# FFN weights of a decoder block: most loaded straight into SBUF with a cast instead of being converted in DRAM first, and bias sums placed ahead of their expansion

## The chip, the cores and the metric

The kernel runs on all eight cores of one Trainium2 chip, one batch element a core. The metric is the device time of the slowest core in microseconds (us). Cores 0 to 3 are one die, cores 4 to 7 the other. The profiles name the engines PE (TensorE, the matmuls), PEld (its weight loads), DVE (VectorE), ACT (ScalarE), POOL (GpSimd) and SP (SyncE).

Some executions fall into a slower state: one die shows a lower granted TensorE clock and runs more than 1% longer than the other, or the time is more than 1.5% above the fastest of that kernel. These executions are marked slow, and only fast ones are compared here.

## The reference, cut to what matters

```python
# BATCH 8, SEQ 2048, D_MODEL 1024, D_FF 4096; all float32
h = rms_norm(x, norm_mix_pre)
u_a, v_a, q, k, v_b, g_a, g_b = split(h @ w_in)
# branch A: chunked spatial gating, 8 groups of 128 channels, chunks of 128 tokens
v   = layer_norm(gelu(v_a), ln_v_g, ln_v_b)
y_a = gelu(u_a) * (tril(w_s) @ v  per chunk and group  + b_s)
# branch B: y_b = dilated sliding-window attention (untouched by the change)
merged = sigmoid(g_a + b) * (y_a @ w_a_proj) + sigmoid(g_b + b) * (y_b @ w_b_proj)
x = x + rms_norm(merged @ w_out)                      # "output projection"
x = x + rms_norm(relu(rms_norm(x) @ w_ff1)**2 @ w_ff2)   # FFN: FF1, then FF2
```

Of the kernel before, what the change touches and what calls it, by code (L numbers as in the profile page):

```python
# [9 lines left out]
BF16 = mybir.dt.bfloat16  # L10
AF = mybir.ActivationFunctionType
ALU = mybir.AluOpType
# [346 lines left out]
def build_nc():  # L359
    nc = bass.Bass("TRN2", target_bir_lowering=False)  # L360
# [21 lines left out]
    vscr_d = nc.dram_tensor("v_scr", [4, 4, 128, 4, 384], BF16).ap()  # L382
    x1_d = nc.dram_tensor("x1_scr", [16, 128, DM], F32).ap()
    gscr_d = nc.dram_tensor("gc_scr", [16, 128, 1024], BF16).ap()
    w1s_d = nc.dram_tensor("w1_bf", [8, 128, 4096], BF16).ap()
    w2s_d = nc.dram_tensor("w2_bf", [16, 128, 2048], BF16).ap()

    es = ExitStack()
    P = Plan(nc, es)
    psall = es.enter_context(nc.psum_tensor("pst", [128, 8, 512], F32))  # L390

    def ps(b):
        return psall[:, b, :]
# [6 lines left out]
    def buf(name, off, shape, dt=BF16):  # L400
        return Buf(P, name, int(off), shape, dt)
# [101 lines left out]
    for i in range(2):  # L503
        P.dve(lambda e, i=i: e.memset(stg[i][:, :, :, 64:128], 1.0), 2048, [], [stg[i].key()], prio=-1950 + i)


    def conv_items():
        its = []
        for f in range(2, 8):
            its.append(lambda f=f: P.dma("pool", lambda e: e.dma_start(out=w1s_d[f], in_=w1_d[f]), 3e6, f"cv{f % 2}", [], [P.nkey(("w1s", f))], after=anchor[0]))  # L510
        for f in range(16):
            its.append(lambda f=f: P.dma("pool", lambda e: e.dma_start(out=w2s_d[f], in_=w2_d[f]), 1.5e6, f"cv{f % 2}", [], [P.nkey(("w2s", f))], after=anchor[0]))
        return its

# [192 lines left out]

    conv = conv_items()
    nconv = len(conv)
    proj_qk(0, lambda i, n: -1990.0 + 20 * i)  # L710
# [26 lines left out]
    wva = buf("wva", 144 * K, [8, 1024])  # L737
    wu = [buf(f"wu{i}", (128 + 2 * i) * K, [8, 128]) for i in range(8)]
    Rx = buf("Rx", 160 * K, [8, 512], F32)
# [75 lines left out]
    for hf in range(2):  # L815
        P.pe([(ps(4 + hf), onesf[:], wsTf[:, 512 * hf:512 * hf + 512], True, True, 2048, False)], [onesf.key(), wsTf.key()], [4 + hf])
        for gi in range(4):
            g = 4 * hf + gi
            o = Rx[:, g, :].rearrange("p (t b m) -> p t b m", t=16, b=4)
            P.dve(lambda e, g=g, gi=gi, hf=hf: e.scalar_tensor_tensor(  # L820
                out=BS[:, 128 * g:128 * g + 128], in0=ps(4 + hf)[:, 128 * gi:128 * gi + 128], scalar=small[:, lb_c + g:lb_c + g + 1],
                in1=BS[:, 128 * g:128 * g + 128], op0=ALU.mult, op1=ALU.add), 128, [ksm, BS.key()], [BS.key((128 * g, 128 * g + 128))], [4 + hf])
            P.dve(lambda e, g=g, o=o: e.tensor_copy(
                out=o, in_=BS[:, 128 * g:128 * g + 128].rearrange("p (t m) -> p t m", t=16).unsqueeze(2).broadcast_to([128, 16, 4, 8])), 512,
                [BS.key((128 * g, 128 * g + 128))], [Rx.key(g)])

# [6 lines left out]
    for g in range(8):  # L833
# [8 lines left out]
        anchor[0] = P.ops[-1]  # L842
        conv.pop(0)()
        for n4 in range(4):
# [24 lines left out]

    def load_w1(f, prio):  # L870
        src = w1_d if f < 2 else w1s_d
        P.dma("pool", lambda e: e.dma_start(out=w1[f][:].rearrange("p k c -> p (k c)"), in_=src[f]), 1e6 if f > 1 else 2e6, f"w1_{f}",
              [P.nkey(("w1s", f))], [w1[f].key()], prio=prio)
    for cb in range(8):
# [9 lines left out]
        for w in range(4):  # L884
# [8 lines left out]
            anchor[0] = P.ops[-1]  # L893
            if conv and cb >= 1 and it % 3:
                P.prio = G0 + 20 * cb + 5 * w + 2
                conv.pop(0)()
            P.prio = G0 + 20 * cb + 5 * w
            s_ = sg[it % 2]
# [73 lines left out]

    for f in range(2, 8):
        load_w1(f, F0 + 4 * (f - 2))
    for q in range(16):
        P.dma("pool", lambda e, q=q: e.dma_start(out=w2[:, 2 * q:2 * q + 2, :].rearrange("p f c -> p (f c)"), in_=w2s_d[q]), 0.5e6, f"w2_{q}",
              [P.nkey(("w2s", q))], [w2.key((2 * q, 2 * q + 2))], prio=F0 + 20 + q, after=fgate[q])
    assert not conv
    gfin = buf("gfin", 200 * K, [1024], F32)
# [5 lines left out]
    for w in range(4):  # L985
        for fb in range(32):
            P.prio = L0 + 100 * w + fb
            f, f4 = fb // 4, fb % 4
            bk = (6, 7)[fctr[0] % 2]
            fctr[0] += 1  # L990
            P.pe([(ps(bk), w1[f][:, kc, 128 * f4:128 * f4 + 128], h2T[:, kc, 512 * w:512 * w + 512], kc == 0, kc == 7, 512, False)
                  for kc in range(8)], [w1[f].key(), h2T.key(None, (512 * w, 512 * w + 512))], [bk], name="ff1")
            P.act(lambda e, fb=fb, bk=bk: e.activation(out=hid[:, fb, :], in_=ps(bk), func=AF.Relu), 512, [], [hid.key(fb)], [bk])  # L993
            P.dve(lambda e, fb=fb: e.tensor_tensor(out=hid[:, fb, :], in0=hid[:, fb, :], in1=hid[:, fb, :], op=ALU.mult), 512, [hid.key(fb)],  # L994
                  [hid.key(fb)], rate=2)
# [116 lines left out]
```

## The kernel before: the parts that the change and the argument touch

A small planner (`P`) records every operation with a priority, and each engine then executes its operations in a fixed order. `P.dma("pool", ...)` goes into GpSimd's queue, which carries every transfer with a cast here; `P.dma("sp", ...)` goes into SyncE's queue. `after=op` holds a transfer back until that operation is done.

The FFN weights w1 (8 chunks, each 1 MB in bf16) and w2 (16 chunks, each 0.5 MB in bf16) arrive as f32. Chunks 2 to 7 of w1 and all of w2, 22 in all, are first converted from DRAM to DRAM and later loaded as bf16:

```python
for f in range(2, 8):
    its.append(lambda f=f: P.dma("pool", lambda e: e.dma_start(out=w1s_d[f], in_=w1_d[f]), ..., after=anchor[0]))
for f in range(16):
    its.append(lambda f=f: P.dma("pool", lambda e: e.dma_start(out=w2s_d[f], in_=w2_d[f]), ..., after=anchor[0]))
```

The stage before gating computes v for 16 tiles of 128 tokens. Each LayerNorm result goes through one of three `gct` buffers into a DRAM scratch, and from there a gather turns it into `gc`, 8 partitions a tile. Both are in SyncE's queue:

```python
for n in range(16):
    ...  # v_a matmuls on PE, gelu on ACT, statistics and normalisation on DVE/POOL
    t_ = gct[n % 3]
    P.dve(... out=t_ ...)
    P.dma("sp", ... e.dma_start(out=gscr_d[n], in_=t_[:]) ...)                       # store, 256 KB
for n in range(16):
    P.dma("sp", ... e.dma_start(out=gc[8*n:8*n+8, :, :],
                                in_=gscr_d[n].rearrange("(b m) c -> m b c", m=8)) ...)   # gather, 256 KB
```

The bias sums `BS` free the PSUM banks 4 and 5, which the first u matmuls need. Each sum was followed by its expansion into `Rx`:

```python
for g in ...:
    P.dve(... scalar_tensor_tensor(out=BS[g], in0=ps(4 + hf)..., in1=BS[g]) ...)
    P.dve(... tensor_copy(out=Rx[g], in_=BS[g] broadcast) ...)
```

Then come u, gating and merge. One conversion is issued per u group, and the other 14 in the merge:

```python
for g in range(8):
    for w in range(4):
        ...                                     # u matmuls, gelu
    anchor[0] = P.ops[-1]
    conv.pop(0)()                               # one conversion
    for n4 in range(4):
        P.prio = U0 + 10 * (g + 3) + 5 + n4     # gating matmuls run about three u groups later
        P.pe(... gc x wsT ...)
for cb in range(8):                             # merge
    P.dma("pool", ... wb <- wg_d[cb], prio=G0 + 20 * cb - 30)
    if cb == 1: ...                             # four loads of w_out
    for w in range(4):
        ...                                     # 32 matmuls
        if conv and cb >= 1 and it % 3: conv.pop(0)()
```

The output projection works through 16 tiles, each with a load of x (512 KB), 16 matmuls, an RMSNorm, a store of x1 (512 KB) and a transpose for the FFN. The bf16 FFN weights are loaded meanwhile:

```python
for i in range(16):
    P.dma("sp", ... x_ <- x[i])                 # two buffers
    ...
    P.dma("sp", ... x1_d[i] <- x_)
for f in range(2, 8): load_w1(f, F0 + 4 * (f - 2))
for q in range(16):   P.dma("pool", ... w2[q] <- w2s_d[q], after=fgate[q])   # after projection tile q
```

The softmax here doesn't subtract the row's maximum and nothing guards it: scores larger than these inputs give would overflow.

## Time and profile before

| | before |
|---|---|
| time, median of 3 runs | 1314.57 us (1313.46 to 1316.37) |
| spans of the eight cores in the profiled execution | 1299.2 to 1318.6 us |
| mean granted TensorE clock of the cores | 0.963 to 0.969 |
| first v_a matmul to first gating matmul, mean of the cores | 185.8 us |
| first gating matmul to first matmul of the projection | 258.7 us |
| first matmul of the projection to first FF2 matmul | 141.4 us |
| first FF2 matmul to the end | 394.3 us |

The last four rows cut the kernel at points that every core has, taken from the trace's records of single matmuls; all cores reach the first v_a matmul at 324 to 329 us. FF1 of the first window begins before the first FF2 matmul, so the third row contains a little of the FFN.

First the table by stage, kernel before, core 3 (the slowest). Each row is a stretch of time; its columns are the length, then the busy us and the instruction count of PE, PE's weight loads, VectorE, ScalarE and GpSimd, then the granted TensorE clock, the mean busy share of the 16 DMA engines, and GB/s.

```profile
core 3: us, PE busy (x) PEld busy (x) DVE busy (x) ACT busy (x) POOL busy (x), PEclk, DMA share, GB/s
415.00:440.00 25.00, 13.42 (x55) 5.40 (x53) 5.38 (x10) 4.94 (x9) 1.96 (x5) 0.80 0.75 132
...
450.00:475.00 25.00, 20.27 (x94) 9.02 (x92) 5.53 (x10) 7.46 (x13) 5.48 (x12) 0.98 0.94 167
475.00:500.00 25.00, 0.00 (x0) 0.00 (x0) 0.00 (x0) 0.00 (x0) 0.00 (x0) 0.50 0.85 126
500.00:517.00 17.00, 0.00 (x0) 0.00 (x0) 0.00 (x0) 0.00 (x0) 0.00 (x0) 0.50 0.44 81
564.00:780.00 216.00, 216.00 (x1004) 97.92 (x1002) 70.77 (x105) 42.65 (x63) 13.38 (x26) 1.00 0.57 91
780.00:900.00 120.00, 99.72 (x524) 46.18 (x523) 75.86 (x123) 66.55 (x185) 9.66 (x18) 0.96 0.73 245
924.00:1255.00 331.00, 329.95 (x1528) 149.43 (x1528) 73.77 (x156) 78.05 (x168) 0.00 (x0) 1.00 0.11 39
```

PE is full in the merge (564 to 780) and in the FFN (924 to 1255). From 475 to 517 it does nothing at all, while the DMA engines are 85% and then 44% busy. The projection (780 to 900) leaves it idle for 20 us of 120.

The chain of work that ended last, same core, tells what the idle time waits for. Columns: start, duration, what.

```profile
414.55 23.25 DMA gc_scr<-sb_gct_127
...
438.86 9.48 DMA gc_scr<-sb_gct_127
448.88 12.46 DMA gc_scr<-sb_gct_129
461.82 39.22 DMA gc_scr<-sb_gct_128
...
501.17 0.27 SPq L808
501.52 7.13 DMA gc_scr<-sb_gct_127
508.78 8.31 DMA sb_gc<-gc_scr
...
786.00 7.54 DMA x_scr<-sb_xo_159
793.66 5.49 DMA sb_xo_159<-x
```

`gc_scr<-sb_gct` are stores of 256 KB; one of them took 39.22 us. The stretch in which PE stands still runs from this store to `sb_gc<-gc_scr`, the last gather. The three buffers explain only a part of why one store follows the other: for the last store (501.52) VectorE had its tile ready at 472.25 (timeline of core 3). The waits of PE from 385 to 565 us on core 3 (total us, times, longest) put numbers on it:

```profile
PE pst L195 <- DMA sb_gc<-gc_scr: 47.3, 1, 47.3
PE pst L195 <- ACT sb_gv_125 L787: 11.3, 2, 10.3
PE pst L195 <- DVE sb_BS L820: 9.0, 1, 9.0
```

PE waits 47.3 us for the gathers, 10.3 us at once for a gelu (held up, through the gct buffers, by a store), and 9.0 us for the bias sums. From 764 to 935 us, in the projection, its wait for a tile of x is small:

```profile
PE pst L195 <- DVE sb_xo_159 L950: 3.9, 2, 2.1
```

### The profile page before, as it was taken

The page shows a single profiled execution, that of the slowest core. Times are in us where ns is not written, and L with a number is a line of the kernel's source. Part 1 is how long each engine was busy: PE and PEld are TensorE (multiplying, and loading weights), DVE is VectorE, ACT ScalarE, POOL GpSimd, SP SyncE. Part 2 cuts the span into 40 slices and gives each one's busy share as a digit, 9 for nine tenths or more (in the row PEclk, how much of TensorE's full clock was granted, in tenths as well). Part 3 has the DMA queues.
Part 4 walks back from the last instruction along what each step waited for, and adds up shares of the span by engine and source line. Part 5 has one row for each costly group of instructions (what it writes and reads, how often), then busy time and mean ns, then how long its engine had stood idle before and what let it go on. Part 6 is the DMA issues. An engine that isn't in the chain of part 4 may idle for free.

```text
span 1318.6 us, 20421 instructions; the slowest of 8 cores (1299.2 to 1318.6 us)
## 1 busy us (share of the span) xinstructions
PE 1174.5 (89%) x7560; PEld 591.2 (45%) x7560; DVE 579.4 (44%) x997; ACT 509.6 (39%) x878; POOL 59.8 (5%) x120
## 2 busy tenths in 40 slices
PE   4799999998985722999999987899999999999997
PEld 2466666554542311544444443444444444444443
DVE  5767777877655401653223336672122113113212
ACT  5357778878643210211221134563123113212311
POOL 0000000000012100000000000010000000000000
PEclk9899999999998865999999998999999999999999
DMA  9474434344118693698645336664020020011001
GB/s 238 130 172 89 91 70 110 87 108 82 25 51 161 127 156 60 84 143 126 96 81 86 75 113 228 218 226 173 33 86 11 9 89 33 0 64 65 1 32 64
DMA packets 63555, 128.32 MB, mean 97 GB/s; under 512 B 37153, under 2 KB 37281, under 8 KB 60962
## 3 DMA queue, kind: packets, MB, share of 16 engines
q0 software_dynamic: 9440, 52.43, 22.5%
q1 hardware_dynamic: 54018, 74.58, 19.4%
q8 instruction: 62, 1.02, 0.3%
q14 instruction: 35, 0.29, 0.1%
HBM read 137.48 MB, written 41.94 MB: 136 GB/s over the span
## 4 chain that ended last, share of the span: by engine, by line
PE 75%; DMA 14%; ACT 4%; DVE 4%; issue 3%; SPq 0%; DVEq 0%; ACTq 0%
PE pst L195 75%; DMA gc_scr<-sb_gct_128 4%; DMA gc_scr<-sb_gct_127 3%; DMA sb_xo_159<-x 2%; DMA sb_xo_160<-x 1%; DMA sb_gc<-gc_scr 1%; DMA gc_scr<-sb_gct_129 1%; DMA sb_xt_87<-x 1%; DMA sb_xt_89<-x 1%; ACT sb_Et_84 L628 1%; DMA sb_wva<-w_va 1%; DMA x_scr<-sb_xo_159 1%; ACT sb_Et_83 L628 1%; ACT sb_Lr_86 L699 0%; PE pst L199 0%
## 5 line engine op out<-in xcount | busy, mean ns | idle before, releaser
L195 PE MATMUL pst<-sb_w_157,sb_hid 128*128 128x512 bf16 x1024 | 221.7, 379 | 2.7 <-DVE sb_hid L994 1.4
L195 PEld LDWEIGHTS pst<-sb_w_157,sb_hid 128*128 128x128 bf16 x1024 | 100.0, 98 | 124.0 <-issue 3.7
L993 ACT ACTIVATE sb_hid<-pst 128x512 bf16<-128x512 f32 x128 | 76.3, 596 | 127.0 <-PE pst L195 126.7
L994 DVE TENSOR_TENSOR sb_hid<-sb_hid 128x512 bf16<-128x512 bf16 x128 | 54.2, 424 | 131.3 <-ACT sb_hid L993 128.8
L1007 ACT ACTIVATE sb_junk_173<-pst 128x512 bf16<-128x512 f32 x32 | 19.1, 598 | 197.3 <-PE pst L195 197.3
L195 PE MATMUL pst<-sb_wva,sb_hT 128*128 128x512 bf16 x256 | 60.8, 391 | 14.9 <-ACT sb_gv_125 L787 11.3
L195 PE MATMUL pst<-sb_wout,sb_merged 128*128 128x512 bf16 x256 | 61.8, 398 | 7.2 <-DVE sb_xo_159 L950 3.9
L195 PE MATMUL pst<-sb_hT,sb_wqk_62 128*128 128x512 bf16 x256 | 65.3, 404 | 0.9 <-DVE sb_hT L496 0.9
L628 ACT ACTIVATE sb_Et_82<-pst 128x1024 bf16<-128x1024 f32 (+1 forms) x54 | 52.4, 970 | 26.3 <-PE pst L195 19.7
L195 PE MATMUL pst<-sb_hT,sb_wqk_63 128*128 128x512 bf16 x256 | 60.4, 380 | 0.0
L195 PE MATMUL pst<-sb_hT,sb_wg_140 128*128 128x512 bf16 x256 | 58.4, 379 | 0.0
L195 PE MATMUL pst<-sb_hT,sb_wg_141 128*128 128x512 bf16 x256 | 57.9, 379 | 0.0
L628 ACT ACTIVATE sb_Et_83<-pst 128x1024 bf16<-128x1024 f32 (+1 forms) x53 | 51.9, 980 | 8.3 <-PE pst L195 4.8
L628 ACT ACTIVATE sb_Et_84<-pst 128x1024 bf16<-128x1024 f32 (+1 forms) x53 | 51.5, 972 | 9.3 <-PE pst L195 6.1
L195 PE MATMUL pst<-sb_wsT,sb_gc 128*128 128x128 bf16 x128 | 9.9, 230 | 47.9 <-DMA sb_gc<-gc_scr 47.3
L840 ACT ACTIVATE sb_yaT<-pst 128x512 bf16<-128x512 f32 x32 | 19.1, 597 | 86.4 <-PE pst L195 86.4
L195 PEld LDWEIGHTS pst<-sb_wva,sb_hT 128*128 128x128 bf16 x256 | 24.3, 100 | 46.2 <-issue 21.0
L195 PEld LDWEIGHTS pst<-sb_wout,sb_merged 128*128 128x128 bf16 x256 | 25.4, 102 | 40.1 <-issue 14.3
L900 ACT ACTIVATE sb_sg_0_145<-pst,sb_small 128x512 f32<-128x512 f32 x16 | 11.0, 688 | 73.1 <-PE pst L195 65.8
L195 PEld LDWEIGHTS pst<-sb_hT,sb_wqk_62 128*128 128x128 bf16 x256 | 24.2, 103 | 33.0 <-issue 12.1
L852 DVE SCALAR_TENSOR_TENSOR sb_tmpm_131<-pst,sb_small,sb_Rx 128x512 bf16<-128x512 f32 x16 | 12.0, 748 | 61.2 <-PE pst L195 61.2
L195 PEld LDWEIGHTS pst<-sb_hT,sb_wg_141 128*128 128x128 bf16 x256 | 25.1, 98 | 30.2
(402 smaller groups left out, 1961.7 us busy)
## 6 DMA issues: line engine op xcount, KB each, us to landing
w_bf<-w POOLq DMA_DIRECT2D x16, 512.0 KB, 12.0
sb_w_157<-w_bf POOLq DMA_DIRECT2D x16, 512.0 KB, 6.2
w_bf<-w POOLq DMA_DIRECT2D x6, 1024.0 KB, 27.4
sb_xo_159<-x SPq DMA_DIRECT2D x8, 512.0 KB, 6.5
sb_gc<-gc_scr SPq DMA_DIRECT2D x16, 256.0 KB
sb_xo_160<-x SPq DMA_DIRECT2D x8, 512.0 KB, 6.1
sb_wg_140<-w_g POOLq DMA_DIRECT2D x4, 1024.0 KB, 12.8
sb_wg_141<-w_g POOLq DMA_DIRECT2D x4, 1024.0 KB, 10.2
```

The costliest lines, as they stand in the source:

```text
L195: e.matmul(out, lhsT=l, rhs=r, start=st, stop=sp, skip_group_check=True))
L628: P.act(lambda e: e.activation(out=et[:, :, 0:W], in_=psall[:, sb:sb + 2, 0:W], func=AF.Exp, scale=0.125), 2 * W, [], [et.key()], [sb, sb ...
L840: P.act(lambda e, bk=bk, g=g, w=w: e.activation(out=yaT[:, g, 512 * w:512 * w + 512], in_=ps(bk), func=AF.Gelu_apprx_tanh), 512, [], [yaT. ...
L852: P.dve(lambda e, bk=bk, g=g, tm=tm: e.scalar_tensor_tensor(out=tm[:], in0=ps(bk), scalar=small[:, lg_c + g:lg_c + g + 1], in1=Rx[:, g, :] ...
L900: P.act(lambda e, j=j, cb=cb, po=po, s_=s_: e.activation(out=s_[j][:], in_=ps(po + j), func=AF.Tanh, scale=0.5, bias=small[:, bg_c + 8 * j ...
L993: P.act(lambda e, fb=fb, bk=bk: e.activation(out=hid[:, fb, :], in_=ps(bk), func=AF.Relu), 512, [], [hid.key(fb)], [bk])
L994: P.dve(lambda e, fb=fb: e.tensor_tensor(out=hid[:, fb, :], in0=hid[:, fb, :], in1=hid[:, fb, :], op=ALU.mult), 512, [hid.key(fb)], [hid.k ...
L1007: P.act(lambda e, hf=hf, bb=bb, s_=s_: e.activation(out=junk4[:, 0:512], in_=ps(bb[hf]), func=AF.Square, accum_out=s_[:, 8 + hf:9 + hf]), ...
```

## The change

The intent was to take conversions out of the stage before gating, where the stores of gct seemed to suffer from them. Chunks 2, 3, 4 of w1 and 0 to 9 of w2 are loaded from f32 into SBUF with the cast, during the output projection. Only nine chunks (w1 5 to 7, w2 10 to 15) are still converted in DRAM, in the merge. The last six w2 chunks are loaded in the first FF1 pass. All BS sums come early, and the copies into Rx later; the places of the u weights in SBUF are permuted to suit.

```diff
-        conv.pop(0)()                                   # in the u/gating loop
+    conv = []
+    for f in range(3):  conv.append(... w1s_d[f] <- w1_d[5 + f] ...)
+    for q in range(6):  conv.append(... w2s_d[q] <- w2_d[10 + q] ...)
...
-            if conv and cb >= 1 and it % 3:             # merge
+            if conv and cb >= 1 and it % 2:
...
-    for f in range(2, 8):
-        load_w1(f, F0 + 4 * (f - 2))                    # bf16
-    for q in range(16):
-        P.dma("pool", ... w2[q] <- w2s_d[q], prio=F0 + 20 + q, after=fgate[q])
+    for n, f in enumerate((2, 3, 4)):
+        load_w1(f, F0 + 8 * n, fgate[n])                # f32, cast
+    for q in range(10):
+        load_w2(q, F0 + 24 + q, fgate[3 + q])           # f32, cast
+    for f in (5, 6, 7):
+        load_w1(f, F0 + 40 + f)                         # bf16
...
+            if w == 0 and fb >= 18 and fb < 24:         # first FF1 pass
+                load_w2(fb - 8, P.prio, P.ops[-1])      # bf16
...
             P.dve(... scalar_tensor_tensor(out=BS[g] ...)
-            P.dve(... tensor_copy(out=Rx[g], in_=BS[g]))
+                prio=M0 + 2)
+    for g in range(8):
+        P.dve(... tensor_copy(out=Rx[g], in_=BS[g]) ..., prio=M0 + 70 + g)
```

More of the change, by code (lines that the diff above doesn't have):

```diff
@@ L383, in build_nc @@
     x1_d = nc.dram_tensor("x1_scr", [16, 128, DM], F32).ap()
+    w1s_d = nc.dram_tensor("w1_bf", [3, 128, 4096], BF16).ap()
+    w2s_d = nc.dram_tensor("w2_bf", [6, 128, 2048], BF16).ap()
     gscr_d = nc.dram_tensor("gc_scr", [16, 128, 1024], BF16).ap()
-    w1s_d = nc.dram_tensor("w1_bf", [8, 128, 4096], BF16).ap()
-    w2s_d = nc.dram_tensor("w2_bf", [16, 128, 2048], BF16).ap()
     es = ExitStack()
@@ L504, in build_nc @@
         P.dve(lambda e, i=i: e.memset(stg[i][:, :, :, 64:128], 1.0), 2048, [], [stg[i].key()], prio=-1950 + i)
-    def conv_items():
-        its = []
-        for f in range(2, 8):
-            its.append(lambda f=f: P.dma("pool", lambda e: e.dma_start(out=w1s_d[f], in_=w1_d[f]), 3e6, f"cv{f % 2}", [], [P.nkey(("w1s", f))], after=anchor[0]))
-        for f in range(16):
-            its.append(lambda f=f: P.dma("pool", lambda e: e.dma_start(out=w2s_d[f], in_=w2_d[f]), 1.5e6, f"cv{f % 2}", [], [P.nkey(("w2s", f))], after=anchor[0]))
-        return its
     T = 100.0
@@ L706, in pv_class @@
                   [ybT.key(hp, (512 * c, 512 * c + 512), rows=(lo, lo + 64))], [bks[hh]], name="norm")
-    conv = conv_items()
-    nconv = len(conv)
     proj_qk(0, lambda i, n: -1990.0 + 20 * i)
@@ L737, in build_nc @@
     wva = buf("wva", 144 * K, [8, 1024])
-    wu = [buf(f"wu{i}", (128 + 2 * i) * K, [8, 128]) for i in range(8)]
+    wu = [buf(f"wu{i}", o * K, [8, 128]) for i, o in enumerate((132, 134, 140, 142, 128, 130, 136, 138))]
     Rx = buf("Rx", 160 * K, [8, 512], F32)
@@ L818, in build_nc @@
             g = 4 * hf + gi
-            o = Rx[:, g, :].rearrange("p (t b m) -> p t b m", t=16, b=4)
             P.dve(lambda e, g=g, gi=gi, hf=hf: e.scalar_tensor_tensor(
                 out=BS[:, 128 * g:128 * g + 128], in0=ps(4 + hf)[:, 128 * gi:128 * gi + 128], scalar=small[:, lb_c + g:lb_c + g + 1],
-                in1=BS[:, 128 * g:128 * g + 128], op0=ALU.mult, op1=ALU.add), 128, [ksm, BS.key()], [BS.key((128 * g, 128 * g + 128))], [4 + hf])
-            P.dve(lambda e, g=g, o=o: e.tensor_copy(
-                out=o, in_=BS[:, 128 * g:128 * g + 128].rearrange("p (t m) -> p t m", t=16).unsqueeze(2).broadcast_to([128, 16, 4, 8])), 512,
-                [BS.key((128 * g, 128 * g + 128))], [Rx.key(g)])
+                in1=BS[:, 128 * g:128 * g + 128], op0=ALU.mult, op1=ALU.add), 128, [ksm, BS.key()], [BS.key((128 * g, 128 * g + 128))], [4 + hf],
+                prio=M0 + 2)
+    for g in range(8):
+        o = Rx[:, g, :].rearrange("p (t b m) -> p t b m", t=16, b=4)
+        P.dve(lambda e, g=g, o=o: e.tensor_copy(
+            out=o, in_=BS[:, 128 * g:128 * g + 128].rearrange("p (t m) -> p t m", t=16).unsqueeze(2).broadcast_to([128, 16, 4, 8])), 512,
+            [BS.key((128 * g, 128 * g + 128))], [Rx.key(g)], prio=M0 + 70 + g)
     for g in range(8):
@@ L868, in build_nc, with load_w1, load_w2 @@
     G0 = 1000.0
-    def load_w1(f, prio):
-        src = w1_d if f < 2 else w1s_d
-        P.dma("pool", lambda e: e.dma_start(out=w1[f][:].rearrange("p k c -> p (k c)"), in_=src[f]), 1e6 if f > 1 else 2e6, f"w1_{f}",
-              [P.nkey(("w1s", f))], [w1[f].key()], prio=prio)
+    conv = []
+    for f in range(3):
+        conv.append(lambda f=f: P.dma("pool", lambda e: e.dma_start(out=w1s_d[f], in_=w1_d[5 + f]), 3e6, f"cv{f % 2}", [],
+                                      [P.nkey(("w1s", 5 + f))], after=anchor[0]))
+    for q in range(6):
+        conv.append(lambda q=q: P.dma("pool", lambda e: e.dma_start(out=w2s_d[q], in_=w2_d[10 + q]), 1.5e6, f"cv{(q + 1) % 2}", [],
+                                      [P.nkey(("w2s", 10 + q))], after=anchor[0]))
+    def load_w1(f, prio, after=None):
+        src = w1_d[f] if f < 5 else w1s_d[f - 5]
+        P.dma("pool", lambda e: e.dma_start(out=w1[f][:].rearrange("p k c -> p (k c)"), in_=src), 2e6 if f < 5 else 1e6, f"w1_{f}",
+              [P.nkey(("w1s", f))], [w1[f].key()], prio=prio, after=after)
+    def load_w2(q, prio, after=None):
+        src = w2_d[q] if q < 10 else w2s_d[q - 10]
+        P.dma("pool", lambda e: e.dma_start(out=w2[:, 2 * q:2 * q + 2, :].rearrange("p f c -> p (f c)"), in_=src),
+              1e6 if q < 10 else 0.5e6, f"w2_{q}", [P.nkey(("w2s", q))], [w2.key((2 * q, 2 * q + 2))], prio=prio, after=after)
     for cb in range(8):
@@ L893, in build_nc @@
             anchor[0] = P.ops[-1]
-            if conv and cb >= 1 and it % 3:
+            if conv and cb >= 1 and it % 2:
                 P.prio = G0 + 20 * cb + 5 * w + 2
                 conv.pop(0)()
-            P.prio = G0 + 20 * cb + 5 * w
+                P.prio = G0 + 20 * cb + 5 * w
             s_ = sg[it % 2]
@@ L970, in build_nc @@
                                                        func=AF.Copy), 1024, [], [kh], [bk])
-    for f in range(2, 8):
-        load_w1(f, F0 + 4 * (f - 2))
-    for q in range(16):
-        P.dma("pool", lambda e, q=q: e.dma_start(out=w2[:, 2 * q:2 * q + 2, :].rearrange("p f c -> p (f c)"), in_=w2s_d[q]), 0.5e6, f"w2_{q}",
-              [P.nkey(("w2s", q))], [w2.key((2 * q, 2 * q + 2))], prio=F0 + 20 + q, after=fgate[q])
-    assert not conv
+    for n, f in enumerate((2, 3, 4)):
[4 more added lines that the diff above has]
+        load_w1(f, F0 + 40 + f)
     gfin = buf("gfin", 200 * K, [1024], F32)
```

## The prediction

> **What bounds the kernel now.** In the table by stage (core 3, span 1318.6 us) PE is busy 216.0 of 216 us in the merge (564 to 780) and 330 of 331 us in the FFN (924 to 1255): PE-bound. Two stages are not: in spatial gating (400 to 517) PE works 52.7 of 117 us, in the output projection (780 to 900) 99.7 of 120.
>
> In gating the chain of waits runs through DMA: gct stores of 256 KB landing in 23.3, 9.5, 12.5, 39.2 and 7.1 us, then the gather of gc, 8.3 us. The first such store took 2.0 us. The waits show PE idle 47.3 us before the first gating matmul (517.55), and 10.3 us before 433 for a gelu held up by a gct buffer not yet stored. All eight cores show this chain.
>
> The culprit is in the issues: FFN conversions DRAM to DRAM at 413.7 and two at 464.9 (median 27.4 us to land), beside wg loads at 455.6 and 456.2 and wout at 463.8 and 470.8. The store issued at 461.8 landed at 501, about when that backlog was gone.
>
> **Cost of a transfer.** From queue shares: a cast load costs about 6.5 us of all 16 engines per MB written (attention: 14.3% of 264 us for 5.77 MB); a conversion the same (700 to 745: 6.3); a bf16 load 3.0 (780 to 924: 28.5% of 144 us for 13.58 MB). So a w1 chunk costs 6.9 us converted, 6.9 direct, 3.2 from bf16; w2 half. [...]
>
> **What changes.**
> 1. Gating: three conversions (21 us of DMA) vanish before the gate; the remaining nine run in the PE-bound merge and hide. wg and wout stay, so a backlog of 14 to 21 us still meets the last stores.
> 2. BS sums first: PE waited 9.0 us for banks 4/5 (395.5 to 404.5); most of that goes. The Rx copies (8 x 0.42 us) leave the LayerNorm chain.
> 3. Output projection: w1 2 to 4 and ten w2 are now f32 loads. Estimate: weight DMA work 64 instead of 41 us in 144, share 0.65 to about 0.81. The x loads (6 us), already in the chain there, get longer: about 0.5 us a tile, 16 tiles.
> 4. Six late w2 loads in the first FF1 pass: 1.6 us each, 9 us of slack: free.
>
> **On the critical path.** Without the stalls the last v_a matmul moves from 454 to about 434 (the LayerNorm chain runs at 2.6 to 2.95 us a tile). From there the wg/wout backlog plus the last store and gather take about 28 us: first gating matmul near 462, saving about 55 us (45 to 65). The projection gives back about 8 (0 to 20). Merge and FFN stay. Sum: 1314.6 - 55 + 8 = 1268 us.
>
> Predicted 1268 us, 8 in 10 within 1246 to 1290. Faster by over 2%: 0.87; same 0.12; slower 0.01.
>
> **What would show each step.** First gating matmul at 455 to 475; gct stores mostly under 10 us; no conversion before 560; PE wait for gc under 25 us, for BS under 3; merge still 216 us at full PE; the stretch from 780 to FFN longer by 0 to 20 us with higher DMA share; FFN unchanged, no wait of FF2 for w2.
>
> **What would make it wrong.** wg loads alone starve the last stores as before (saving only 30); f32 weight loads starve x loads in the projection (loss over 20); w1 5 to 7 or w2 10 to 15 land late and FFN waits; or the static order shifts so that u matmuls no longer fill the wait.

1314.6 - 55 + 8 = 1268 us (1267.6 before rounding).

## The result, and the profile after

| | before, same job | after |
|---|---|---|
| median | 1314.86 us (1313.46 to 1316.37, 4 runs) | 1328.48 us (1327.24 to 1397.54, 4 runs, the last one slow) |
| ratio of fast runs | | 1.010, 95% interval 1.008 to 1.012 |

A ratio is the mean time of one kernel's fast runs over that of the other's in the same rounds, so it is not quite the ratio of the medians. The kernel was expected at 1268 us and came out 1% slower than before, within the 2% that count as the same. The mean stretches of the eight cores, from the records of the matmuls:

| us, mean of the cores | before | after | difference | predicted |
|---|---|---|---|---|
| first v_a to first gating matmul | 185.8 | 163.7 | -22 | about -55 |
| first gating matmul to projection | 258.7 | 263.9 | +5 | 0 |
| projection to first FF2 | 141.4 | 166.9 | +25.5 | +8 |
| first FF2 to end | 394.3 | 394.3 | 0 | 0 |

The second row hides two populations: 255.2 to 256.0 us on cores 0, 1, 6 and 7, and 271.6 to 273.2 us on cores 2 to 5. The view of cores (span, mean granted clock) shows the same split:

```profile
core 1: 1303.9 us, clock 0.965
...
core 3: 1323.3 us, clock 0.948
...
core 5: 1325.7 us, clock 0.950
...
core 7: 1312.6 us, clock 0.964
```

The table by stage after, core 5 (the slowest):

```profile
core 5: us, PE busy (x) PEld busy (x) DVE busy (x) ACT busy (x) POOL busy (x), PEclk, DMA share, GB/s
415.00:440.00 25.00, 15.40 (x62) 6.43 (x61) 9.41 (x17) 6.06 (x12) 2.96 (x8) 0.78 0.68 121
...
450.00:475.00 25.00, 20.04 (x77) 8.07 (x75) 4.70 (x8) 5.97 (x10) 3.78 (x8) 0.78 0.91 163
475.00:500.00 25.00, 4.94 (x25) 2.97 (x26) 4.04 (x8) 0.00 (x0) 0.00 (x0) 0.51 0.38 77
500.00:517.00 17.00, 17.00 (x91) 8.27 (x89) 8.78 (x17) 4.25 (x8) 0.54 (x1) 0.81 0.18 31
...
770.00:890.00 120.00, 94.55 (x481) 43.40 (x480) 68.31 (x113) 62.11 (x176) 7.74 (x15) 0.91 0.79 198
890.00:931.00 41.00, 31.13 (x154) 14.04 (x152) 12.36 (x23) 13.02 (x24) 4.08 (x8) 0.92 0.67 217
931.00:1262.00 331.00, 329.95 (x1528) 149.43 (x1528) 73.70 (x155) 78.03 (x168) 0.00 (x0) 1.00 0.11 39
```

Between 475 and 500 PE is still nearly idle. From 500 on it is full again, but at a clock of 0.81: 91 matmuls in 17 us. A busy PE at 0.81 still reads as fully busy, which is why the column PEclk must be read beside it. The FFN row is unchanged.

The chain of work that ended last, core 5:

```profile
417.26 16.16 DMA gc_scr<-sb_gct_127
433.93 9.00 DMA gc_scr<-sb_gct_129
...
454.13 14.36 DMA gc_scr<-sb_gct_128
468.97 18.90 DMA gc_scr<-sb_gct_127
487.99 6.61 DMA sb_gc<-gc_scr
...
776.31 12.95 DMA x_scr<-sb_xo_159
789.39 8.56 DMA sb_xo_159<-x
...
903.38 16.15 DMA sb_w_7_156<-w_bf
```

The 39 us store is gone, but the stores are still slow: 16.16, 14.36 and 18.90 us, with no conversion anywhere near. The last store is still held in SyncE's queue behind a gather, for 16.2 us on the mean of the cores. In the projection the store of x1 and the load of x that stood in the chain have grown (7.54 to 12.95, and 5.49 to 8.56 us), and there is a new wait for w1 chunk 7. Its load is issued behind the w2 loads in GpSimd's order, and landed 16.15 us after 903.38.

The waits of PE on core 5, from 385 to 565 us:

```profile
PE pst L195 <- DMA sb_gc<-gc_scr: 25.0, 1, 25.0
PE pst L195 <- ACT sb_gv_125 L776: 9.6, 1, 9.6
...
PE pst L195 <- DVE sb_BS L808: 0.7, 1, 0.7
```

And those on the same core from 764 to 935 us:

```profile
PE pst L195 <- DVE sb_xo_159 L954: 16.7, 5, 11.3
...
PE pst L195 <- DMA sb_w_7_156<-w_bf: 8.4, 1, 8.4
```

The wait for the bias sums fell from 9.0 to 0.7 us as intended, and the wait for the gathers from 47.3 to 25.0 us. The wait of 9.6 us for a gelu stayed. The wait for the tile of x (`sb_xo_159`) was 3.9 us before (core 3, the same stretch) and is 16.7 us now. The wait of 8.4 us for w1 chunk 7, a bf16 load, is new (4.8 to 8.4 us on the eight cores).

So there are three questions: why gating won 22 us and not 55, why the projection gave back 25 us and not 8, and what the clock does.

### The profile page after: what moved, and what is told of

Same layout as the page of the kernel before. It is cut to its first block, busy times and chain, and to the rows that moved or that the text cites. A ratio compares the mean times of both kernels' runs of the same rounds, so it can differ in the third digit from the quotient of the medians.

```text
span 1325.7 us, 20381 instructions; the slowest of 8 cores (1303.9 to 1325.7 us)
## 1 busy us (share of the span) xinstructions
PE 1198.5 (90%) x7560; PEld 598.2 (45%) x7560; DVE 578.5 (44%) x997; ACT 508.8 (38%) x878; POOL 53.7 (4%) x107
## 4 chain that ended last, share of the span: by engine, by line
PE 77%; DMA 13%; ACT 4%; DVE 3%; issue 2%; SPq 0%; POOL 0%; DVEq 0%; ACTq 0%; POOLq 0%
PE pst L195 77%; DMA gc_scr<-sb_gct_127 3%; DMA x_scr<-sb_xo_159 2%; DMA sb_xo_159<-x 2%; DMA gc_scr<-sb_gct_129 1%; DMA sb_w_7_156<-w_bf 1%; DMA gc_scr<-sb_gct_128 1%; DMA sb_gc<-gc_scr 1%; DMA sb_xt_87<-x 1%; ACT sb_Et_84 L619 1%; DMA sb_wva<-w_va 1%; DMA sb_w_5_154<-w_bf 1%; PE pst L199 1%; ACT sb_Et_83 L619 1%; ACT sb_Lr_86 L690 0%
## 5 line engine op out<-in xcount | busy, mean ns | idle before, releaser
L999 ACT ACTIVATE sb_hid<-pst 128x512 bf16<-128x512 f32 x128 | 76.3, 596 | 138.6 <-PE pst L195 138.2
L195 PE MATMUL pst<-sb_wout,sb_merged 128*128 128x512 bf16 x256 | 63.4, 402 | 20.9 <-DVE sb_xo_159 L954 16.7
L195 PE MATMUL pst<-sb_wva,sb_hT 128*128 128x512 bf16 x256 | 63.6, 405 | 12.7 <-ACT sb_gv_125 L776 9.6
L195 PE MATMUL pst<-sb_hT,sb_wqk_62 128*128 128x512 bf16 x256 | 65.8, 407 | 0.9 <-DVE sb_hT L496 0.9
L619 ACT ACTIVATE sb_Et_82<-pst 128x1024 bf16<-128x1024 f32 (+1 forms) x54 | 52.4, 970 | 26.5 <-PE pst L195 19.9
L195 PE MATMUL pst<-sb_hT,sb_wg_140 128*128 128x512 bf16 x256 | 61.4, 393 | 0.0
L195 PE MATMUL pst<-sb_hT,sb_wg_141 128*128 128x512 bf16 x256 | 60.8, 393 | 0.0
L195 PE MATMUL pst<-sb_hT,sb_wqk_63 128*128 128x512 bf16 x256 | 60.4, 380 | 0.0
L195 PEld LDWEIGHTS pst<-sb_wout,sb_merged 128*128 128x128 bf16 x256 | 25.5, 103 | 54.7 <-issue 30.3
L195 PEld LDWEIGHTS pst<-sb_hT,sb_wg_141 128*128 128x128 bf16 x256 | 25.7, 101 | 32.5 <-issue 9.8
L904 ACT ACTIVATE sb_sg_0_145<-pst,sb_small 128x512 f32<-128x512 f32 x16 | 11.0, 688 | 74.9 <-PE pst L195 68.8
L195 PEld LDWEIGHTS pst<-sb_hT,sb_wqk_62 128*128 128x128 bf16 x256 | 24.4, 103 | 33.2 <-issue 12.6
L195 PEld LDWEIGHTS pst<-sb_hT,sb_wg_140 128*128 128x128 bf16 x256 | 25.5, 101 | 30.6 <-issue 8.0
L904 ACT ACTIVATE sb_sg_0_143<-pst,sb_small 128x512 f32<-128x512 f32 x16 | 11.0, 688 | 73.2 <-PE pst L195 68.0
## 6 DMA issues: line engine op xcount, KB each, us to landing
sb_gc<-gc_scr SPq DMA_DIRECT2D x16, 256.0 KB
```

The lines of the kernel that those rows point to most:

```text
L195: e.matmul(out, lhsT=l, rhs=r, start=st, stop=sp, skip_group_check=True))
L619: P.act(lambda e: e.activation(out=et[:, :, 0:W], in_=psall[:, sb:sb + 2, 0:W], func=AF.Exp, scale=0.125), 2 * W, [], [et.key()], [sb, sb ...
L904: P.act(lambda e, j=j, cb=cb, po=po, s_=s_: e.activation(out=s_[j][:], in_=ps(po + j), func=AF.Tanh, scale=0.5, bias=small[:, bg_c + 8 * j ...
L999: P.act(lambda e, fb=fb, bk=bk: e.activation(out=hid[:, fb, :], in_=ps(bk), func=AF.Relu), 512, [], [hid.key(fb)], [bk])
```

## The experiments

Theory A for gating: the gathers are the next limit. Each writes only 8 partitions, and the traces show them on about half of the 16 DMA engines: while nothing but the last two gathers is under way, the mean share of the engines is 0.55 (core 3 before, 510 to 515 us; 0.53 on core 5 after, 490 to 492 us), against 1.01 when the last store runs beside other transfers (core 3 before, 502.55 to 503.05 us). Each also stands in SyncE's queue ahead of later stores (two effects, which the runs below do not fully part). The packets of 4 bytes in SyncE's queue fit: the last two gathers show 16 of them (core 3 before, from 509 us), and between 385 and 497 us on core 5 after there are 448, which is 16 stores x 16, plus 16 gathers x 8, plus 64 for four other transfers. That a gather runs on exactly 8 engines, as the expectations below have it, is an estimate from these numbers (0.55 of 16 is 8.8). Rival A1: the conversions' large packets, not the gathers, were the trouble. Rival A2: the bias part matters more than the conversions. Rival A3: the weights of the merge (two wg chunks and w_out), loaded early, hold up the last stores.

Theory B for the projection: the f32 loads give back what gating won. Theory C: the clock step of 0.81 costs about 17 us on the cores that have it, whatever the weights do.

In all, 16 runs were made in four jobs, each beside the kernel before on the same chip; the ratios below are against it. The word "stretches" means the mean stretches defined above.

### 1. All conversions kept, but moved into the merge

```diff
-(after) w1 2-4 and w2 0-9 direct; 9 conversions, `if conv and cb >= 1 and it % 2`
+all 22 conversions, `if conv and it >= 2 and it % 5`; projection loads bf16 as in the kernel before
```

> The changed kernel with all 22 conversions kept, but every one in the merge, and the output projection loading bf16 as before. Theory 1 (the f32 weight loads in the output projection give back what gating gained): from first output-projection matmul to first FF2 matmul back to 138-148 us (changed kernel 162-171), gating as in the changed kernel (first v_a to first gating matmul 160-167 us), merge still without PE waits; so about 1293-1300 us if the clock stays at full, about 1305 if four cores drop to 0.81 again. Rival (the longer projection comes from the earlier start or the static order, not from the f32 loads): that stretch stays above 160 us and the total near 1325 us.

Measured: 1303.76 us median (1297.87 to 1311.58, 4 runs, one counted as slow), ratio 0.9904 (0.9838 to 0.9971). Stretches: 165.4, then 255.4 (cores 2 to 5) or 272.3 (cores 0, 1, 6, 7, at a clock of 0.81), then 142.1 us. The projection returns to what it was before (142.1 against 141.4), so its loss in the changed kernel belongs to the direct f32 loads. The gating stretch is that of the changed kernel (165.4 against 163.7). And the clock step is there too, in every one of the four executions, each time on another pair or pairs of cores.

### 2. Bias part alone

```diff
 (before)
-BS sum, Rx copy, BS sum, Rx copy ...; wu places 128 + 2 i
+BS sums first (prio M0 + 2), Rx copies later (prio M0 + 70 + g); wu places permuted
```

> The kernel before with only the bias reordering and the new wu places. If the gating gain comes from the conversions leaving (theory), first v_a to first gating matmul stays at 180-188 us (before 184) and the total within 5 us of before (1310-1317). If the bias reordering is what gained, it falls to 164 and the total to about 1295. PE wait for BS should fall from 9 us to under 3 in both.

Measured: 1315.08 us (1313.66 to 1317.17), ratio 1.0007 (0.9969 to 1.0045). Stretches 185.3, 255.4, 143.7 us. Beside the conversions the bias part does not move the first gating matmul. The wait for BS is gone from the waits of cores 0 and 3, but the longest wait for a gelu is 14.7 and 15.4 us there (10.3 on core 3 before), and the wait for the gathers 42.7 and 43.0 us: what was won in front is waited for behind. Behind it 3.3 us are won and 2.3 us lost again in the projection. Rival A2 falls for this setting.

### 3. As experiment 1, without the bias part

```diff
 (experiment 1)
-BS sums first, Rx copies later, wu places permuted
+BS sum, Rx copy, BS sum ... as before
```

> Run e1 without the bias reordering and with the old wu places: only the conversions moved from gating to the merge. If the conversions' leaving is the gain, first v_a to first gating matmul is 160-172 us and the total within 6 us of e1. If the bias part is needed for it, above 178 us. Also a look at the clock: does the 0.81 step come without the bias part.

Measured: 1297.7 us (1293.12 to 1389.48, one slow), ratio 0.9873 (0.9813 to 0.9933). Stretches 168.1, 258.8, 140.3 us. No core at 0.81 in the profile. The bias part is worth 2.7 us in the first stretch and 3.4 in the second once the conversions are out, read from the cores at full clock; the totals of experiments 1 and 3 cannot be compared directly, since the former carries the clock step.

### 4. The changed kernel with gathers onto 16 partitions

```diff
 (after)
-gscr_d = dram_tensor([16, 128, 1024]);   store out=gscr_d[n]
-16 gathers: out=gc[8n : 8n+8], in_=gscr_d[n].rearrange("(b m) c -> m b c", m=8)
+gscr_d = dram_tensor([16, 8, 16, 1024]); store out=gscr_d[n].rearrange("m b c -> b m c")
+8 gathers:  out=gc[8n : 8n+16], in_=gscr_d[n:n+2].rearrange("n m b c -> (n m) (b c)")
```

> The changed kernel with the scratch of gct laid out by target partition and gathered two tiles at a time: 8 gathers onto 16 partitions, rows of 32 KB, instead of 16 gathers onto 8 partitions. Theory 2 (what is left of the gating wait is the gathers themselves, which run on 8 of the 16 engines and hold up the stores behind them): first v_a to first gating matmul falls from 164 to 140-152 us, the v_a wait of 10 us at about 420 goes, total 1305-1315. Rival (the wg and wout backlog of 21 us after the last v_a matmul decides): it falls by less than 6 us, total above 1320.

Measured: 1297.78 us (1295.61 to 1300.16), ratio 0.9874 (0.9836 to 0.9913). Stretches 148.5, 252.1, 168.8 us; no 0.81. The new gathers alone take 15 us from the gating stretch of the changed kernel (163.7 to 148.5), and the total is below the 1305 to 1315 us expected. SyncE's queue shows 416 packets of 4 bytes, as 16 x 16 for the stores, 8 x 16 for the gathers and 32 for two others would give. The stores in the chain of core 0 are each shorter than the store at the same place in the changed kernel's chain, least so the last two, beside the merge's weights:

```profile
410.64 10.08 DMA gc_scr<-sb_gct
...
421.24 8.60 DMA gc_scr<-sb_gct
...
430.40 7.29 DMA gc_scr<-sb_gct
...
438.30 12.72 DMA gc_scr<-sb_gct
...
451.96 14.67 DMA gc_scr<-sb_gct
```

The edit changes three things: the number of engines (by the packets of 4 bytes, 16 a gather instead of 8), the length of the rows (32 KB instead of 2 KB), and the number of gathers (8 instead of 16), so that SyncE's queue stops half as often for a store to land. Experiment 5 takes out the rows alone.

### 5. Long rows alone, still onto 8 partitions

```diff
 (experiment 1)
-gscr_d [16, 128, 1024]; gather in rows of 2 KB
+gscr_d [16, 8, 16, 1024]; gather in rows of 32 KB, still 16 gathers, each out=gc[8n : 8n+8]
```

> e1 with the scratch laid out by target partition as in e6 (rows of 32 KB), but still 16 gathers onto 8 partitions; PE's order is that of e1. Tells what made the pairs of e4 and e6 faster. If it is that a gather onto 8 partitions runs on 8 engines (theory): first v_a to first gating matmul 160-172 us as in e1 (165)[...]. If it is the long rows: 145-152 us as in e6.

Measured: 1298.95 us (1296.12 to 1301.02), ratio 0.9881 (0.9849 to 0.9914). Stretches 167.9, 255.3, 142.2 us. The gating stretch does not shorten (165.4 in experiment 1). So it is not the rows that help. What is left is the partitions, that is, by the estimate above, the engines, together with the number of gathers; no run changes one of these without the other. The timelines show both at work. A store of the sixth tile is issued just behind the gathers of the first four tiles, the same 1 MB in both layouts; from its issue to that of the gather that waits for it pass 18.0 us here and 10.6 us in experiment 6 (mean of the cores), which speaks for the engines. And all 16 stores together are held in SyncE's queue, after their tiles are ready, for 42.6 us here and 17.3 us in experiment 6. From the packet records an estimate: the gathers' packets in the changed kernel take about 420 us in sum (645.6 us of 2048-byte packets in SyncE's queue, less 226 for the stores, as experiment 4 shows them alone). On 8 engines, the estimate above, that is 52 us each, within some 90 us.

### 6. Both: conversions in the merge, gathers onto 16 partitions

```diff
 (experiment 1)
+the gathers and the scratch of experiment 4
```

> e1 and e4 together: all 22 conversions in the merge, bf16 loads in the output projection, gathers in pairs. If the two losses are separate, the gains add: first v_a to first gating matmul 146-151 us, output projection to FF2 137-147 us, total 1268-1280 us. If they share a cause (less idle time in gating wakes the clock step, say), the total stays above 1285 us. With the 10 us v_a wait shortened, no core should show 0.81 (none did in e4; four did in e1).

Measured: 1273.46 us (1268.23 to 1425.14, one slow), ratio 0.964 (0.9606 to 0.9674). Stretches 147.8, 251.7, 143.8 us; no 0.81. Counted from the changed kernel, the gains of experiments 1 and 4 add up. This is the base for experiments 7 to 9.

### 7. Direct f32 loads of w1 2 to 4 alone

```diff
 (experiment 6)
-w1 2, 3, 4 converted in the merge, loaded as bf16
+w1 2, 3, 4 loaded from f32 with a cast, after projection tiles 0, 1, 2
```

> e6 with one part of the change put back: w1 chunks 2, 3 and 4 loaded as f32 right after the merge, all w2 from bf16. If the three w1 loads alone, 21 us of DMA in the first 20 us of the output projection, are most of the loss: output projection to FF2 152-165 us, total 12-20 us over e6. If the ten f32 w2 loads spread over the projection are the loss: under 147 us, total within 5 us of e6.

Measured: 1286.43 us (1284.57 to 1380.08, one slow), ratio 0.9747 (0.9724 to 0.9769), 13 us more than experiment 6. Only the third stretch grows, 143.8 to 157.7 us.

### 8. Direct f32 loads of w2 0 to 9 alone

```diff
 (experiment 6)
-w2 0 to 9 converted in the merge, loaded as bf16
+w2 0 to 9 loaded from f32 with a cast, after projection tiles 0 to 9
```

> e6 with the ten w2 chunks loaded as f32 in the output projection, all w1 as in e6. If the two kinds of f32 loads add up to the loss (e4 minus e6 is 24 us in the time, and the three w1 loads of e7 are 13 of it): output projection to FF2 150-157 us, total 8-13 us over e6. If w1 was all of it: within 3 us of e6.

Measured: 1283.58 us (1282.06 to 1285.55), ratio 0.9762 (0.9728 to 0.9796). Experiment 6 ran in another job, so the ratios are to be compared: 0.0122 of some 1315 us is about 16 us more (10 by the medians; 8 to 13 were expected). Third stretch 156.6 us.

The two extra costs in the third stretch, 13.9 and 12.8 us, sum to 26.7; both together cost 25.0 (experiment 4 against 6, 168.8 less 143.8). The waits of PE for the tile of x from 727 us on, core 0, first in experiment 6:

```profile
PE pst L195 <- DVE sb_xo L950: 6.0, 4, 2.5
```

The same wait in experiment 7:

```profile
PE pst L195 <- DVE sb_xo L950: 24.2, 6, 15.0
```

And in experiment 8:

```profile
PE pst L195 <- DVE sb_xo L950: 20.3, 5, 7.7
```

The cost is a handful of waits, the longest 15.0 us, and not half a microsecond a tile. That two x buffers cannot carry PE over an x1 store and an x load that land late one after the other is a reading of the chain; no run gave x a third buffer. Theory B is shown, and by halves. The wait for late bf16 chunks of w1, w1 7 above all, needs both kinds of f32 loads: 6.3 us on core 0 in experiment 4, none there in experiments 7 and 8 (at most 1.6 us on any core).

### 9. Merge weights held back

```diff
 (experiment 6)
-wg chunks 0 and 1 and w_out issued as their buffers come free
+wg chunks 0 and 1 and w_out issued after the first gating matmul (after=gate1)
```

> e6 with wg0, wg1 and wout issued only after the first gating matmul has begun to wait no more (they wait for it). If the backlog of these cast loads is what is left of the wait for gc (about 18 us in e4), the first gating matmul comes 10-16 us earlier than in e6 and the total is 1258-1268 us. If the gathers alone set it, under 4 us. The merge must not wait for wg: 14 us of loads in 40 us.

Measured: 1292.91 us (1282.99 to 1461.64; two of the four executions slow), no interval. First stretch 135.1 us, 12.7 us less than experiment 6, and PE waits 11.7 us for the gathers on core 0, where it waits 19.0 us in experiment 6. So rival A3 holds beside theory A: the early loads of the merge's weights are the next part of the missing gain. The total did not show it, because four cores ran the merge at 0.81: 284.3 us against 257.4 us on the others, and the spans of the cores without the step are 1250 to 1260 us. All four executions had the step on some cores.

### 10. Merge weights held back and gating two groups later

```diff
 (experiment 9)
-P.prio = U0 + 10 * (g + 3) + 5 + n4
+P.prio = U0 + 10 * (g + 5) + 5 + n4
```

> e10 with the first gating matmuls two channel groups later in PE's order (after u5, not u3), so that PE has u matmuls to do while it waits for gc and does not stop at 456-461 us. Theory on the clock: the step to 0.81, held some 161 us, comes a few us after PE stands still and starts again on all cores; then no core shows it here, and the total is 1250-1265 us. Rival: what sets it off is load alone; then four cores show 0.81 as in e10 and the total is 1275-1295 us.

Measured: 1264.72 us (1260.21 to 1455.55, one slow), ratio 0.9611 (0.9573 to 0.9649). Stretches 138.2, 250.2, 145.2 us. PE no longer waits for the gathers at all (no such line among the waits of cores 0 and 3), and no core is at 0.81 in the profile. It is the fastest version.

### 11. The kernel before with conversions in short rows

```diff
 (before)
-w1s_d [8, 128, 4096], w2s_d [16, 128, 2048]: conversions in packets of 32 KB
+w1s_d [8, 256, 2080], w2s_d [16, 128, 2080], 2048 of 2080 columns used: rows of 4 KB
```

> The kernel before with the same conversions at the same places, but in rows of 4 KB (scratch rows padded so that they do not merge) instead of 32 KB runs; PE's order is the same. If the gct stores wait because a conversion's packet holds an engine for 4.2 us, the longest store falls from 39 to under 28 us and first v_a to first gating matmul from 184 to 165-176 us. If only the volume matters, it stays at 180-188 us and the total within 5 us of before.

Measured: 1309.77 us (1305.42 to 1311.94), ratio 0.9924 (0.9891 to 0.9958). The packets became 4096 bytes (324 ns each in the median, instead of 3.5 us from 385 to 520 us and 4.2 us from 470 to 520 us on core 3 before) and PE's order stayed the same. The first stretch is 182.6 us and PE waits 41.5 us for the gathers on core 0, where it waits 41.9 us in the kernel before. The longest time from the issue of a store to that of its gather is 33 to 38 us on the eight cores, against 38 to 43 before; under 28 had been the mark for large packets as the cause. Rival A1 falls for the missing gain: the size of the conversions' packets is worth about 3 us in this stretch and 0.8% of the total.

### 12. The kernel before with gathers onto 16 partitions

```diff
 (before)
+the gathers and the scratch of experiment 4, nothing else
```

> The kernel before with only the gathers in pairs; conversions, bias and loads untouched. If the gathers on 8 engines hold up the stores with or without conversions: v_a wait of 10 us gone, first v_a to first gating matmul 166-174 us instead of 184, total 1300-1308 us. If the conversions decide alone as long as they are there: above 180 us, total as before.

Measured: two fast runs at 1293.36 and 1293.46 us, two slow at 1345.16 and 1409.72; ratio of fast runs 0.9841 (0.9797 to 0.9884). First stretch 158.4 us (166 to 174 expected), so the new gathers alone win 27.4 us with all conversions in place, more than removing the conversions wins (22.1, or 19.9 in experiment 13). With the new gathers already in place, removing them is worth only another 10 us (158.4 to 148.5).

### 13. The changed kernel again, unedited

> The changed kernel, unedited, in six executions of a second job. Theory: the clock step to 0.81 on some pairs of cores is a matter of the single execution, and where it falls it costs about 16.7 us on those cores (272.3 - 255.6 us between the first gating matmul and the first of the projection). Executions with a core at a mean clock of 0.955 or less then take 1320 to 1330 us, those without take 1308 to 1317 us, and the ratio to the kernel before lies between 0.995 and 1.012. Rival: the step belongs to the change and comes on cores 2 to 5 in every fast execution, with the ratio at 1.008 to 1.012 again. Second rival: the step costs nothing in all, because the core that ends last is another one; executions with and without it then agree within 4 us.

Measured: 1312.55 us median (1309.47 to 1329.15, 6 runs), ratio 0.9972 (0.9947 to 0.9998). Five executions took 1309.5 to 1313.6 us with no core below a mean clock of 0.961. The sixth, counted as slow, took 1329.15 us with cores 4 and 5 at 0.948 and 0.949 (spans 1325.0 and 1327.6; the other cores 1301.3 to 1310.1). Stretches of the profiled execution, which is free of the step: 165.9, 255.3, 164.7 us. So the first theory holds: the step belongs to the execution, and costs about 17 us where it falls. The rival, always the same cores, falls, and so does the rival that it costs nothing.

The waits of PE from 385 to 565 us on core 7 are close to those of the first job, so the rest of the explanation does not rest on the step:

```profile
PE pst L195 <- DMA sb_gc<-gc_scr: 28.0, 1, 28.0
...
PE pst L195 <- ACT sb_gv L776: 13.2, 2, 11.6
```

### 14. The changed kernel without its bias part

```diff
 (after)
-BS sums first, Rx copies later, wu places permuted
+BS sum, Rx copy, BS sum ... as before
```

> The changed kernel with its bias part taken back (sums and copies of the bias interleaved as before, old places of the weights of the u groups). Of the kernels whose records show 0.81, all have the bias part; the same all-scratch kernel without it (label e9_allbf16_oldbias) never showed it. If the bias part sets the step off: no core at 0.955 or less in any execution, 1308 to 1317 us, 3 to 6 us more between the first gating matmul and the first of the projection than 255.6. If the step has nothing to do with the bias part: cores at 0.955 or less in about as many executions as in f1_after_again, 1318 to 1330 us there. In both cases from the first v_a matmul to the first gating matmul 164 to 169 us, and 165 to 169 us from the projection to the first FF2 matmul.

Measured: 1319.36 us (1318.23 to 1340.64, 6 runs), ratio 1.0026 (0.9999 to 1.0053). Stretches 168.1, 259.0, 165.5 us. One of the six executions, counted as slow, has cores 4 and 5 at 0.944 and 0.946 and takes 1340.64 us: the step occurs without the bias part as well, as often as in experiment 13. The bias part does not set it off. The five others take 1318.2 to 1320.1 us, slightly above the 1308 to 1317 us for executions without the step. Without the conversions in the way the bias part is worth 6.8 us (1319.36 less 1312.55), where it was worth nothing in experiment 2.

### 15. The changed kernel with gating two groups later

```diff
 (after)
-P.prio = U0 + 10 * (g + 3) + 5 + n4
+P.prio = U0 + 10 * (g + 5) + 5 + n4
```

> The changed kernel with each gating group put two u groups later in PE's order; transfers and bytes as they are. Theory: after the change the stage before gating still waits on the gathers' way through half of the engines, and PE has nothing else to do there, so two more u groups (about 14 us of PE work each) fill that wait: the wait of PE for the gathers falls from 25 us to under 8, time from the first v_a matmul to the first matmul of the projection falls by 12 to 24 us, total 1295 to 1312 us. Rival: PE was held by DMA volume that only moves elsewhere, so the total stays within 6 us of f1_after_again.

Measured: 1311.36 us (1309.39 to 1393.5, 6 runs, one slow), ratio 0.9967 (0.994 to 0.9994). A miss for the theory: the wait for the gathers fell only from 27.5 to 19.4 us (core 0), the first two stretches together from 421.2 to 419.1 us, and the total by 1.2 us against experiment 13. The rival, within 6 us, holds. The first gating matmul comes when the gathers have landed, 166.8 us after the first v_a matmul, whatever PE does meanwhile; about 8 us more work was fitted in, and new waits between gating and VectorE (4.8 us for tmpm) took up a part of it.

### 16. Experiment 6 with gating two groups later

```diff
 (experiment 6)
-P.prio = U0 + 10 * (g + 3) + 5 + n4
+P.prio = U0 + 10 * (g + 5) + 5 + n4
```

> e6_allbf16_pairs with each gating group two u groups later, without holding back the merge's weights (so e12_hold_g5 minus the hold). If the order alone gave the gain of e12_hold_g5 over e6_allbf16_pairs: 1260 to 1266 us, ratio 0.957 to 0.964. If the hold is needed for it: 1269 to 1274 us, ratio 0.964 to 0.968. No clock of 0.81 in the profile, if an unbroken PE at the start of gating keeps it off.

Measured: 1273.48 us (1271.31 to 1274.74), ratio 0.9679 (0.9651 to 0.9706). No core at 0.81. Order alone gives nothing here either; it needs the hold of experiment 9, which lets the gathers land earlier. PE still waits 12.8 us for them (core 0).

## Why the prediction was wrong, point by point

**The main step that failed: "Without the stalls the last v_a matmul moves from 454 to about 434".** It moved to 449 us (mean of the cores, profile after; 453 before). The step took the wait for the gelu, and the slow stores behind it, to be the work of the conversions. In the changed kernel, with no conversion before 560 us, PE still waits 9.6 us in one piece for that gelu, and stores still take 16 us. With gathers onto 16 partitions the last v_a matmul comes at 446 us with all conversions in place (experiment 12), and at 439 us without them (experiments 4 and 6); no run reaches 434. What the runs put in the step's place is a third user of the DMA engines which the prediction never costed: the kernel's own gathers, 16 of them on about half of the engines (a share of 0.55), each of which can also hold SyncE's queue until its store has landed. It named "the culprit" from which transfers stood beside the slow stores, and the gathers stand beside every store.

**The same step's sequel, "the wg/wout backlog plus the last store and gather take about 28 us", was mis-sized too.** The time from the last v_a matmul to the first gating matmul is 41.5 us after (58.8 before), 35.0 in experiment 6, and 22.7 when the wg and w_out loads are held back (experiment 9). Here the mechanism was named and its size was off. Against the 50.7 us between the kernel before (185.8) and experiment 9 (135.1), in the order in which they were removed: 20.4 us for taking the conversions out of gating together with the bias part (experiment 1), 17.6 for the gathers (experiment 6), 12.7 for the merge's weights. The order matters: with the gathers mended first, they count 27.4 and the conversions with the bias part 10 to 11.

**The term "the projection gives back about 8 (0 to 20)" was mis-sized: it is 23 to 25 us.** Its ingredient was nearly right: 23 us more DMA work was estimated (64 less 41), and about 29 us came, from 0.63 of 147.8 us (core 3 before, the whole stage) to 0.74 of 164.6 us (core 5 after). The step from share to time failed. It let a higher share, 0.81 in 144 us, absorb that work; in the runs the stage grew by 23 to 25 us and the share only to 0.74. And it spread half a microsecond over 16 tiles, where the runs show a few long waits: those for the tile of x, behind a store and then a load of the same buffer, and one of 8.4 us for w1 chunk 7. The prediction had listed both as ways to be wrong ("loss over 20", "w1 5 to 7 or w2 10 to 15 land late and FFN waits"). Experiments 7 and 8 show that w1 and w2 each cause about half.

**"Merge and FFN stay" left out the clock.** PE in the merge is as busy as before, and FFN is unchanged. But in the first job the records of cores 2 to 5 show a clock of 0.812 from 435 to 438 us until 596 or 597 us, broken only by idle time, and this is worth 16.7 us on those cores (272.3 against 255.6). It is the difference between a ratio of 0.997 (experiment 13) and the 1.010 of the first job, and so the reason why the kernel came out on the wrong side of the one before. The other 44 us or so that are missing against the prediction (1312.55 less 1268) are not its doing.

The account without the step, experiment 13 against before, by stretches: -19.9, -3.4, +23.3, 0; the mean over the cores does not move, and the slowest core gains 0.3%. The whole gain of gating is handed back in the projection.

**What was right.** Conversions left gating, and the 39 us store with them. The wait for BS fell below 3 us (0.7), that for the gathers to about 25 us, the edge of what was forecast (27.5 and 28.0 us in experiment 13). FF2 never waited for a late w2 chunk. The first gating matmul was to come at 455 to 475 us, and came at 487 to 495: that was the observation that would have shown the step wrong, and did.

**Not settled.** How the gain of the new gathers divides between the engines and the fewer stops of SyncE's queue is not shown; 16 gathers in a queue of their own would tell. What sets off the clock step stays open. In the records of all three kernels that show it in their profile it begins 2.5 to 7 us after the core's own clock has come back from 0.5 (at 435 to 440 us in the changed kernel and experiment 1, near 469 us in experiment 9), and ends 159 to 161 us later in the changed kernel, though PE stays full there (core 5 after, 173.00 of 173 us busy from 597 to 770 us, at 1.00). But experiments 3 and 5 come back from idle in the same place without it, experiments 4, 6, 7 and 8 from a longer idle time at 475 to 483 us, and experiment 13 had it in one execution of six where the first job had it in all three fast ones. None of the 26 fast executions of the kernel before shows it. That a break of PE just before is needed is therefore only a suspicion; experiment 10, which keeps PE busy there, is free of it in its three fast executions, as are others that do not.

## What to carry to other kernels

Before removing a transfer that stands beside slow ones, cost every transfer that shares the engines with them, the kernel's own small scatter and gather steps first: the gathers onto 8 partitions kept about half of the engines busy here (a share of 0.55), and mending their layout, with half as many gathers, was worth more (27 us) than moving the weight conversions out of the stage (20 to 22 us). A load that can be prepared in a stage bound by PE should not be moved into one that already waits for DMA; here the same chunks were free in the merge (255.4 us with all 22 conversions in experiment 1, 255.6 us with nine after, on cores at full clock) and cost 25 us in the projection. And read the granted clock of every core before comparing two kernels, in more than one job if it differs: one step of it outweighed the whole change.
